# A record-counting kernel: tiles of 384 rows in four slots in place of 512 rows in three, and the last batch's pieces summed before one matmul

## The chip, the cores and the metric

The kernel runs on one core of a Trainium2 chip. The metric is the device time of one execution in microseconds (us). A core has five engines that run their own instruction queues and meet at semaphores: TensorE (PE, matmuls into PSUM), VectorE (DVE), ScalarE (ACT), GpSimd (POOL) and SyncE (SP), which here issues nearly all transfers. The transfers themselves run on 16 DMA engines.

## The reference

```python
B, S, D = 8, 2048, 4096          # x is [B, S, D], w is [D, 1], all float32

def reference(x, w):
    proj = (x @ w).squeeze(-1)
    cm = np.maximum.accumulate(proj, axis=1)
    is_record = (proj >= cm).astype(np.float32)
    return np.cumsum(is_record, axis=1).astype(np.float32)
```

Every row of x (4096 values, 16 KB) is reduced to one dot product with w. Along S, a running maximum says which dot products are records, and a running count of the records is the output, [8, 2048]. x is 268 MB and is read once; everything else is small.

## The kernel before

**Rows in tiles.** The first 1920 of the 2048 positions are worked off in four groups, of 4, 4, 4 and 3 times 128 positions (`RS`, lines 42 to 50). A group has eight tiles, one for each batch, from batch 7 down to batch 0. A tile of a four-row group is 128 partitions by four rows of x, which lie one after the other in memory: 64 KB for each partition, 8 MB in all. In the last group a tile has three rows: 48 KB and 6 MB. The tiles go through `NS` = 3 slots of `xall` (line 81), each wide enough for four rows; tile t of a group uses slot t % 3, in every group anew. All loads are issued by SyncE in one queue, in program order (lines 154 to 173). A load waits, by the semaphore `fr` of the earlier user of its slot, until VectorE and ScalarE are both through with that tile; `user_before` (lines 147 to 150) says which one it is: for t >= 3 the tile t - 3 of the same group, for t < 3 the last tile of the group before that used the same slot, which is tile 6, 7 or 5 for t = 0, 1 or 2.

**Work on a tile.** The columns of a row are split. VectorE takes the first 2816 (`VC`), a multiply with a running sum in one instruction per row (`dot`, line 120; `group_dots`, line 240). GpSimd multiplies the other 1280 with w in place (`group_products`, line 263), and ScalarE adds them up (`add_up`, line 126; `group_sums`, line 278). GpSimd starts on a tile when VectorE has seen it land (`go`). The two partial results of a row and batch are columns of `sum_v` and `sum_p`.

**End of a group.** TensorE turns the columns of both sums into rows of PSUM (`ps`, lines 295 to 305), which adds them at the same time: a matmul with the identity, for each row of the tile one for `sum_p` and one for `sum_v`, once all eight tiles are done. VectorE then runs three instructions (`scans`, line 135): a running maximum from `ps` to `cm`, the comparison (which overwrites `ps`), and a running sum to `cnt`. They stand at the start of the next group's VectorE program (`group_scans`, line 235); a first pass before the first group works on filler values. The loops of VectorE, GpSimd and ScalarE are hardware loops over the first three groups, with the last group written out behind them. The counts of a group are stored from SyncE's queue behind the next group's fifth load (lines 170 to 173).

**The last 128 positions** are loaded as single rows (16 KB for each partition, 2 MB), one for each batch. Batches 7 to 2 are whole rows (`rows`); batches 1 and 0 are cut into nine pieces of columns that get smaller towards the end (`PIECES`, lines 56 to 66). Rows 0 to 2 of this tail go into the fourth row of the three slots, which the last group doesn't use, rows 3 to 5 into the slot of the last group's tile 5, and the pieces into that of tile 6 (`slot`, line 175). The store of the last group's counts stands between the fourth and the fifth piece, and waits for that group's scans. VectorE runs the tail's first dot product, then the last group's scans, then the rest (lines 326 to 338).

**The last matmuls** (lines 340 to 357): three turn the results of batches 7 to 1, and one for each partial result of a piece of batch 0 turns that column (7 from VectorE, 2 from ScalarE), all added in one row set of `ps`. Each matmul waits for its own operand; the two from ScalarE are moved towards the end of the order. A float32 matmul shows as two passes in the profile. Then come the last `scans`, over 128 columns, and the last store.

Of the kernel before, what the change touches and what calls it, by code (L numbers as in the profile page):

```python
# [20 lines left out]
def kernel(  # L21
# [17 lines left out]
    B, S, D = x.shape  # L39
    WC = 512  # L40
    NW = D // WC
    RS = (4, 4, 4, 3)
    R = RS[0]
    NS = 3
    NG = len(RS)
    NL = NG - 1
    N = R * P
    STARTS = [sum(RS[:g]) * P for g in range(NG)]
    S0 = sum(RS) * P
    assert S0 + P == S  # L50
    VC = 2816
    PC = D - VC
    CV = 3584
# [27 lines left out]
    xbuf = [xall[:, i * R * D : (i + 1) * R * D] for i in range(NS)]  # L81
    w_sb = sb([P, PC], "w_sb")
    cm = sb([B, N], "cm")
    cnt = sb([B, N], "cnt")
    cm_l, cnt_l = (sb([B, P], n) for n in ("cm_l", "cnt_l"))
    w_v = wpool.tile([P, CV], FP32, name="w_v")
    ps = wpool.tile([P, WC], FP32, name="ps")
    w_row = w2[:NW, :]
# [8 lines left out]
    sum_v, sum_p = cut(R * B), cut(R * B)  # L97
    st_v, st_p = cut(B), cut(B)
    b1x = cut(B)
    acc_v = cut(len(PIECES))  # L100
    acc_p = cut(len(PIECES))
    neg = cut(1)[:B]

    ns = iter(range(1000))

    def sem(name):
        return tc.alloc_semaphore(f"{name}_{next(ns)}")

    rows = [b for b in reversed(range(B)) if b > 1]
    xs = [sem("xs") for _ in range(B)]  # L110
    fr = [sem("fr") for _ in range(B)]
    xt = [sem("xt") for _ in rows]
    xq = [sem("xq") for _ in PIECES]
    ws, idn, bw, wc, cs, od, oe, psr, pd, pl, go, sd, pa, con = (
# [17 lines left out]
        assert W2 <= c0 and c1 <= W2 + WC  # L132
        return w2[:, c0 - W2 : c1 - W2]

    def scans(cm_, cnt_, n, cm0, cnt0, base=1):
        low = neg.to_broadcast([B, n])
        V.tensor_tensor_scan(  # L137
            out=cm_, data0=ps[:B, :n], data1=low, initial=cm0, op0=ALU.max, op1=ALU.max,
        )._wait_ge(psr, base).then_inc(psr, 1)
        V.tensor_tensor(  # L140
            out=ps[:B, :n], in0=ps[:B, :n], in1=cm_, op=ALU.is_ge
        )._wait_ge(psr, base + 1).then_inc(psr, 1)
        V.tensor_tensor_scan(  # L143
            out=cnt_, data0=ps[:B, :n], data1=low, initial=cnt0, op0=ALU.add, op1=ALU.max,
        )._wait_ge(psr, base + 2).then_inc(cs, 1)

    def user_before(g, t):
        if t >= NS:
            return t - NS, g + 1
        return max(u for u in range(B) if u % NS == t), g  # L150

    with tc.tile_critical(no_gpsimd_drain=True):  # L152

        for g in range(NG):
            r = RS[g]
            for t in range(B):
                i = SY.dma_start(
                    out=xbuf[t % NS][:, : r * D],
                    in_=x[B - 1 - t, STARTS[g] : STARTS[g] + r * P, :].rearrange(
                        "(p r) d -> p (r d)", r=r  # L160
                    ),
                ).then_inc(xs[t], 16)
                u, n = user_before(g, t)
                if n:
                    i._wait_ge(fr[u], 2 * n)
                if g == t == 0:
                    A.dma_start(
                        out=w_row, in_=w.rearrange("(k c) one -> k (c one)", k=NW)
                    ).then_inc(ws, 16)
                if t == 4 and g:  # L170
                    SY.dma_start(
                        out=out[:, STARTS[g - 1] : STARTS[g]], in_=cnt
                    )._wait_ge(cs, g + 1).then_inc(od, 16)

        def slot(m):
            if m < NS:
                return None, xbuf[m][:, RS[-1] * D :]
            u = B - NS if m < 2 * NS else B - NS + 1
            return u, xbuf[u % NS][:, (m % NS) * D : (m % NS + 1) * D]

        freed = {None}

        def row_load(m, c0, c1, b, done):
            u, xb = slot(m)
            i = SY.dma_start(  # L185
                out=xb[:, c0:c1], in_=x[b, S0:, c0:c1]
            ).then_inc(done, 16)
            if u not in freed:
                freed.add(u)
                i._wait_ge(fr[u], 2 * NG)  # L190

        for m, b in enumerate(rows):
            row_load(m, 0, D, b, xt[m])
        for i, (b, c0, c1, _, _) in enumerate(PIECES):
            row_load(B - 1 - b, c0, c1, b, xq[i])
            if i == 3:
                SY.dma_start(
                    out=out[:, STARTS[-1] : S0], in_=cnt[:, : S0 - STARTS[-1]]
                )._wait_ge(cs, NG + 1).then_inc(oe, 16)


# [28 lines left out]
        V.memset(cnt[:, N - 1 :], 0.0)  # L230
        V.wait_ge(con, 3)
        V.wait_ge(wc, 3)
        V.memset(ps[:B, :N], LOW).then_inc(psr, 1)  # L233

        def group_scans(r=R):
            V.wait_ge(od, 16)
            n = r * P
            scans(cm[:, :n], cnt[:, :n], n, cm[:, N - 1 :], cnt[:, N - 1 :])

        def group_dots(r):  # L240
            for t in range(B):
                b, s = B - 1 - t, t % NS
                V.wait_ge(xs[t], 16).then_inc(go, 1)
                V.sem_inc(xs[t], -16)  # L244
                for j in range(r):
                    i = dot(
                        xbuf[s][:, j * D : j * D + VC], w_v[:, :VC],
                        sum_v[:, j * B + b : j * B + b + 1],
                    )
                i.then_inc(fr[t], 1)  # L250

        def next_group():
            group_scans()
            V.sem_inc(psr, -3)
            V.sem_inc(od, -16)

        with V.Fori(0, NL):
            next_group()
            group_dots(R)
        next_group()  # L260
        group_dots(RS[-1])

        def group_products(r):
            for t in range(B):
                s = t % NS
                for j in range(r):
                    xl = xbuf[s][:, j * D + VC : (j + 1) * D]
                    i = G.tensor_mul(out=xl, in0=xl, in1=w_sb).then_inc(pl, 1)  # L268
                    if j == 0:
                        i._wait_ge(go, 1)  # L270
                G.sem_inc(go, -1)  # L271

        G.wait_ge(wc, 3)
        with G.Fori(0, NL):  # L274
            group_products(R)
        group_products(RS[-1])

        def group_sums(r):
            for t in range(B):
                b, s = B - 1 - t, t % NS  # L280
                for j in range(r):
                    i = add_up(
                        xbuf[s][:, j * D + VC : (j + 1) * D],
                        sum_p[:, j * B + b : j * B + b + 1],
                    )._wait_ge(pl, j + 1)
                i.then_inc(fr[t], 1)
                A.sem_inc(pl, -r)
            A.wait_ge(pd, 1)
            A.sem_inc(pd, -1)

        with A.Fori(0, NL):
            group_sums(R)
        group_sums(RS[-1])

        for g, r in enumerate(RS):
            for j in range(r):
                for k, l in enumerate((sum_p, sum_v)):
                    i = T.matmul(  # L298
                        out=ps[:B, j : r * P : r], lhsT=l[:, j * B : (j + 1) * B],
                        rhs=identity, start=k == 0, stop=k == 1,  # L300
                    )
                    if j == k == 0:
                        i._wait_ge(fr[B - 1], 2 * (g + 1))
                    if j == r - 1:
                        i.then_inc((pd, psr)[k], 1)


# [18 lines left out]
        for m, b in enumerate(rows):  # L326
            piece(
                slot(m)[1], (0, VC), (VC, D), st_v[:, b : b + 1], st_p[:, b : b + 1],
                xt[m],
            )  # L330
            if m == 0:
                group_scans(RS[-1])
        for i, (b, c0, c1, v, p) in enumerate(PIECES):
            if b == 1:
                dst_v, dst_p = (b1x if p is None else st_v)[:, 1:2], st_p[:, 1:2]
            else:
                dst_v, dst_p = acc_v[:, i : i + 1], acc_p[:, i : i + 1]
            piece(slot(B - 1 - b)[1], v, p, dst_v, dst_p, xq[i])
            if i == 1:
                parts += [(B, st_v, (sd, nv)), (B, b1x, None), (B, st_p, (pa, na))]  # L340
            elif b == 0:
                parts.append((1, dst_v, (sd, nv)))
                if p:
                    parts.append((1, dst_p, (pa, na)))

        a0 = next(i for i, q in enumerate(parts) if q[2] == (pa, na - 1))
        a1 = next(i for i, q in enumerate(parts) if q[2] == (pa, na))
        parts.insert(len(parts) - 2, parts.pop(a1))
        parts.insert(len(parts) - 4, parts.pop(a0))
        for k, (m, l, wait) in enumerate(parts):  # L350
            i = T.matmul(  # L351
                out=ps[:m, :P], lhsT=l[:, :m], rhs=identity,
# [2 lines left out]
            if wait:  # L355
                i._wait_ge(*wait)
        i.then_inc(psr, 1)
        n = RS[-1] * P
        scans(cm_l, cnt_l, P, cm[:, n - 1 : n], cnt[:, n - 1 : n], 4)
        SY.dma_start(out=out[:, S0:], in_=cnt_l)._wait_ge(cs, NG + 2).then_inc(oe, 16)  # L360
        G.wait_ge(oe, 16 * 2)

# [29 lines left out]
```

## Time and profile before

| what | value |
|---|---|
| median of 8 runs (lowest, highest) | 633.08 us (632.11, 633.44) |
| the profiled execution, its own time | 632.51 us |
| its span, first to last instruction | 630.6 us |
| HBM read over the span | 268.45 MB, 426 GB/s with writes |
| busy: VectorE / GpSimd / ScalarE / PE | 406.0 / 368.8 / 177.7 / 31.9 us |
| loads of four rows, issue to landing (median of the 24) | 44.9 us |
| mean granted TensorE clock | 0.647 |

In the profile, L121 is line 121 of the kernel; that of a helper stands for all its calls, so L121 is every dot product of VectorE and L127 every sum of ScalarE. The granted clock is the share of full speed that TensorE was allowed. The slices cut the span into 40 equal parts and give a busy share in tenths. The chain of waits goes back from the last instruction, at each step to what released it; "issue" in it is time in which the engine waited for nothing that the profile shows. The costliest groups of instructions read: line, engine, operation, written operand, read operands, shapes and count, then busy time and the mean of one in ns, then idle time before and what ended it:

```profile
L121 DVE CUSTOM_DVE_ANT_0 xall<-xall,w_v 128x2816 f32<-128x2816 f32 (+3 forms) x135 | 388.7, 2932 | 189.5 <-DVEq L244 187.4
L268 POOL TENSOR_TENSOR xall<-xall,w_sb 128x1280 f32<-128x1280 f32 x120 | 344.8, 2906 | 248.0 <-POOLq L271 248.0
L127 ACT ACTIVATE xall<-xall 128x1280 f32<-128x1280 f32 x129 | 162.6, 1261 | 432.6 <-POOL xall L268 414.6
```

VectorE and GpSimd each wait some 190 to 250 us in all for tiles (the lines named after the arrow are the semaphore steps that follow a landing), ScalarE for GpSimd's products.

### The profile page before, as it was taken

What the parts mean: (1) busy time and instruction counts of PE and PEld (TensorE: products, weight loads), DVE (VectorE), ACT (ScalarE), POOL (GpSimd) and SP (SyncE); (2) the same over time, 40 slices, a digit from 0 to 9 for tenths busy, and PEclk for the clock granted to TensorE, in tenths of its full rate; (3) what the DMA queues carried; (4) which work ended last, traced back from release to release, by engine and by line L of the source; (5) the groups of instructions that cost most, each with busy time, mean ns of one, the idle gap of its engine ahead of it and who ended that gap; (6) DMA issues with size and microseconds to landing.
All of it is one profiled execution on the core that took longest, in us unless ns stands there. A gap on an engine that the chain in (4) does not pass through costs nothing.

```text
span 630.6 us, 1174 instructions
## 1 busy us (share of the span) xinstructions
PE 31.9 (5%) x100; PEld 14.4 (2%) x100; DVE 406.0 (64%) x291; ACT 177.7 (28%) x262; POOL 368.8 (58%) x137
## 2 busy tenths in 40 slices
PE   8000000000010000000020000000002000000102
PEld 3000000000000000000010000000001000000001
DVE  0755676556785557755579655577557866655797
ACT  1222332123322223322233222332222332232242
POOL 0555676455765557755567655577555766555865
PEclk9999999999965555555555555555556555555556
DMA  9999999999999999999999999999999999999996
GB/s 400 399 466 412 453 399 466 400 466 399 466 412 453 428 436 449 417 453 412 457 407 461 403 466 399 467 399 466 399 459 396 409 446 446 406 446 446 403 428 242
DMA packets 6869, 268.57 MB, mean 426 GB/s; under 512 B 800, under 2 KB 1328, under 8 KB 1872
## 3 DMA queue, kind: packets, MB, share of 16 engines
q1 hardware_dynamic: 6848, 268.50, 98.8%
q14 instruction: 4, 0.03, 0.0%
q8 instruction: 1, 0.02, 0.0%
q10 hardware_dynamic: 16, 0.02, 0.0%
HBM read 268.45 MB, written 0.07 MB: 426 GB/s over the span
## 4 chain that ended last, share of the span: by engine, by line
POOL 52%; issue 37%; DMA 7%; PE 3%; DVE 1%; SPq 0%; POOLq 0%; ACT 0%; ACTq 0%
POOL xall L268 52%; DMA xall<-in_x_dram 6%; PE w_v L215 2%; DVE xall L121 0%; PE ps L215 0%; PE ps L351 0%; DMA w<-in_w_dram 0%; SPq L185 0%; POOLq L271 0%; ACT w L225 0%; DVE cm_l L137 0%; DVE cnt_l L143 0%; DVE ps L140 0%; ACT xall L127 0%; POOLq L274 0%
## 5 line engine op out<-in xcount | busy, mean ns | idle before, releaser
L121 DVE CUSTOM_DVE_ANT_0 xall<-xall,w_v 128x2816 f32<-128x2816 f32 (+3 forms) x135 | 388.7, 2932 | 189.5 <-DVEq L244 187.4
L268 POOL TENSOR_TENSOR xall<-xall,w_sb 128x1280 f32<-128x1280 f32 x120 | 344.8, 2906 | 248.0 <-POOLq L271 248.0
L127 ACT ACTIVATE xall<-xall 128x1280 f32<-128x1280 f32 x129 | 162.6, 1261 | 432.6 <-POOL xall L268 414.6
L298 PE MATMUL ps<-identity,small 128*8 128x128 f32 x60 | 13.2, 412 | 569.1 <-ACT xall L127 569.1
L319 POOL TENSOR_TENSOR xall<-xall,w_sb 128x1280 f32<-128x1280 f32 (+1 forms) x8 | 22.1, 2766 | 6.8 <-DMA xall<-in_x_dram 6.7
L127 ACT ACTIVATION_READ_ACCUMULATOR xall<-xall 128x1 f32 x129 | 24.0, 186 | 0.0
L298 PEld LDWEIGHTS ps<-identity,small 128*8 128x8 f32 x60 | 7.5, 130 | 575.9 <-ACT xall L127 572.0
L137 DVE TENSOR_TENSOR_SCAN cm<-ps,cm,small 8x512 f32<-8x512 f32 (+1 forms) x5 | 6.1, 1217 | 13.2 <-PE ps L298 13.2
L215 PE MATMUL w_v<-w,identity 8*128 8x512 f32 x14 | 12.1, 1056 | 0.0
L233 DVE MEMSET ps<- 8x512 f32 x1 | 0.5, 485 | 17.2 <-ACT w L225 17.2
L121 DVE DVE_READ_ACCUMULATOR2_ANT small<- 128x1 f32 x135 | 11.0, 81 | 0.0
L143 DVE TENSOR_TENSOR_SCAN cnt<-ps,cnt,small 8x512 f32<-8x512 f32 (+1 forms) x5 | 6.1, 1217 | 0.2
L351 PE MATMUL ps<-identity,small 128*1 128x128 f32 (+1 forms) x24 | 4.7, 351 | 23.0 <-DVE small L121 23.0
L215 PEld LDWEIGHTS w_v<-w,identity 8*128 8x128 f32 x14 | 4.6, 332 | 7.3 <-issue 7.3
L222 ACT COPY w_sb<-w_v 128x768 f32<-128x768 f32 x1 | 0.8, 799 | 11.4 <-PE w_v L215 11.4
L140 DVE TENSOR_TENSOR ps<-ps,cm 8x512 f32<-8x512 f32 (+1 forms) x5 | 3.3, 660 | 0.2
L351 PEld LDWEIGHTS ps<-identity,small 128*1 128x1 f32 (+1 forms) x24 | 1.8, 93 | 26.2 <-DVE small L121 25.2
L215 PE MATMUL ps<-w,identity 8*128 8x512 f32 x2 | 2.1, 1136 | 2.7 <-DMA w<-in_w_dram 2.7
L221 ACT ACT_TABLE_LOAD x1 | 1.3, 1283 | 1.5 <-SPq L152 1.5
L221 ACT COPY w_sb<-ps 128x512 f32<-128x512 f32 x1 | 0.6, 586 | 2.0 <-PE ps L215 2.0
L137 DVE TENSOR_TENSOR_SCAN cm_l<-ps,cm,small 8x128 f32<-8x128 f32 x1 | 0.5, 470 | 0.7 <-PE ps L351 0.7
L319 POOL TENSOR_TENSOR xall<-xall,w 128x320 f32<-128x320 f32 x1 | 0.9, 863 | 0.0
(14 smaller groups left out, 3.4 us busy)
## 6 DMA issues: line engine op xcount, KB each, us to landing
xall<-in_x_dram SPq DMA_DIRECT2D x8, 6144.0 KB, 32.6
xall<-in_x_dram SPq DMA_DIRECT2D x6, 2048.0 KB, 42.5
xall<-in_x_dram SPq DMA_DIRECT2D x1, 1344.0 KB, 36.8
xall<-in_x_dram SPq DMA_DIRECT2D x2, 384.0 KB, 30.6
xall<-in_x_dram SPq DMA_DIRECT2D x1, 704.0 KB, 38.2
xall<-in_x_dram SPq DMA_DIRECT2D x1, 640.0 KB, 39.2
xall<-in_x_dram SPq DMA_DIRECT2D x24, 44.9
xall<-in_x_dram SPq DMA_DIRECT2D x1, 224.0 KB, 21.9
```

The lines of the kernel that those rows point to most:

```text
L121: return V.tensor_tensor_reduce(out=xsl, in0=xsl, in1=wsl, scale=1.0, scalar=0.0, op0=ALU.mult, op1=ALU.add, accum_out=dst,)
L127: return A.activation(out=xsl, in_=xsl, func=ACTF.Copy, accum_out=dst)
L137: V.tensor_tensor_scan(out=cm_, data0=ps[:B, :n], data1=low, initial=cm0, op0=ALU.max, op1=ALU.max,)._wait_ge(psr, base).then_inc(psr, 1)
L140: V.tensor_tensor(out=ps[:B, :n], in0=ps[:B, :n], in1=cm_, op=ALU.is_ge)._wait_ge(psr, base + 1).then_inc(psr, 1)
L143: V.tensor_tensor_scan(out=cnt_, data0=ps[:B, :n], data1=low, initial=cnt0, op0=ALU.add, op1=ALU.max,)._wait_ge(psr, base + 2).then_inc(cs, 1)
L215: i = T.matmul(out=dst, lhsT=identity[:NW, k : k + 1].to_broadcast([NW, P]), rhs=w_row, start=True, stop=True,).then_inc(bw, 1)
L221: A.copy(out=w_sb[:, CV - VC :], in_=ps)._wait_ge(bw, 1).then_inc(wc, 1)
L222: A.copy(out=w_sb[:, : CV - VC], in_=w_v[:, VC:CV])._wait_ge(bw, NW).then_inc(wc, 1)
L268: i = G.tensor_mul(out=xl, in0=xl, in1=w_sb).then_inc(pl, 1)
L298: i = T.matmul(out=ps[:B, j : r * P : r], lhsT=l[:, j * B : (j + 1) * B], rhs=identity, start=k == 0, stop=k == 1,)
L319: G.tensor_mul(out=xl, in0=xl, in1=w_pool(*p))._wait_ge(landed, 16).then_inc(pl, 1)
L351: i = T.matmul(out=ps[:m, :P], lhsT=l[:, :m], rhs=identity, start=k == 0, stop=k == len(parts) - 1,)
```

## The change

Three things are changed.

1. Tiles have three rows (48 KB for each partition, 6 MB) in all groups, of which there are five, and go through four slots. Tile k of all 40 uses slot k % 4; since eight tiles are a multiple of four, the slot follows from t alone, and a load always waits for the load four back. `xs` and `fr` are one semaphore for each slot. All five groups are passes of the hardware loops. The tail's rows 0 to 2 go into slot 0, rows 3 to 5 into slot 1, the pieces into slot 2.
2. In `scans`, the comparison writes a tile of its own in SBUF (`rec`, `rec_l`) instead of `ps`, and the running sum adds to each element a zero that lies in the last column of `ps`, in place of a maximum with a very low number.
3. The partial results of batch 0's pieces lie in one array, `accs` (18 columns, those not used are zero). VectorE adds them up with one instruction into `fin` after the last piece, and one matmul turns `fin`. In front of the last piece's dot product VectorE waits for ScalarE's last sum.

```diff
-    RS = (4, 4, 4, 3)
-    R = RS[0]
-    NS = 3
-    NG = len(RS)
+    R = 3
+    NS = 4
+    NG = (S - P) // (R * P)
...
+    rec = sb([B, N], "rec")
...
-    acc_v = cut(len(PIECES))
-    acc_p = cut(len(PIECES))
+    accs = cut(2 * len(PIECES))
+    acc_v, acc_p = accs[:, : len(PIECES)], accs[:, len(PIECES) :]
+    fin = cut(1)
     neg = cut(1)[:B]
+    zero = ps[:B, WC - 1 :]
...
         V.tensor_tensor(
-            out=ps[:B, :n], in0=ps[:B, :n], in1=cm_, op=ALU.is_ge
+            out=rec_, in0=ps[:B, :n], in1=cm_, op=ALU.is_ge
         )._wait_ge(psr, base + 1).then_inc(psr, 1)
         V.tensor_tensor_scan(
-            out=cnt_, data0=ps[:B, :n], data1=low, initial=cnt0, op0=ALU.add, op1=ALU.max,
+            out=cnt_, data0=rec_, data1=zero.to_broadcast([B, n]), initial=cnt0,
+            op0=ALU.add, op1=ALU.add,
         )._wait_ge(psr, base + 2).then_inc(cs, 1)
...
+        for k in range(NK):
+            g, t = divmod(k, B)
+            i = SY.dma_start(
+                out=xbuf[k % NS],
+                in_=x[B - 1 - t, g * N : (g + 1) * N, :].rearrange(
+                    "(p r) d -> p (r d)", r=R
+                ),
+            ).then_inc(xs[k % NS], 16)
+            if k >= NS:
+                i._wait_ge(fr[k % NS], 2 * (k // NS))
...
+            if t == NS and g:
+                SY.dma_start(
+                    out=out[:, (g - 1) * N : g * N], in_=cnt
+                )._wait_ge(cs, g + 1).then_inc(od, 16)
...
         def slot(m):
-            if m < NS:
-                return None, xbuf[m][:, RS[-1] * D :]
-            u = B - NS if m < 2 * NS else B - NS + 1
-            return u, xbuf[u % NS][:, (m % NS) * D : (m % NS + 1) * D]
+            return m // R, xbuf[m // R][:, (m % R) * D : (m % R + 1) * D]
...
-        with V.Fori(0, NL):
-            next_group()
-            group_dots(R)
-        next_group()
-        group_dots(RS[-1])
+        with V.Fori(0, NG):
+            group_scans()
+            V.sem_inc(psr, -3)
+            V.sem_inc(od, -16)
             for t in range(B):
...
+            if i == len(PIECES) - 1:
+                V.wait_ge(pa, na)
             piece(slot(B - 1 - b)[1], v, p, dst_v, dst_p, xq[i])
...
-            elif b == 0:
-                parts.append((1, dst_v, (sd, nv)))
-                if p:
-                    parts.append((1, dst_p, (pa, na)))
-
-        a0 = next(i for i, q in enumerate(parts) if q[2] == (pa, na - 1))
-        a1 = next(i for i, q in enumerate(parts) if q[2] == (pa, na))
-        parts.insert(len(parts) - 2, parts.pop(a1))
-        parts.insert(len(parts) - 4, parts.pop(a0))
+        V.tensor_reduce(
+            out=fin, in_=accs, op=ALU.add, axis=mybir.AxisListType.X
+        )._wait_ge(sd, nv).then_inc(sd, 1)
+        nv += 1
+        parts.append((1, fin, (sd, nv)))
+
```

The loops of GpSimd and ScalarE and the matmuls of a group are changed in the same way: one loop over five groups of three rows, and `fr[NS - 1]` as the matmuls' wait.

## The prediction

> **What bounds the kernel now.** I read the slices of the span first, then the DMA queues, then the chain of waits.
>
> ```profile
> DVE  0755676556785557755579655577557866655797
> POOL 0555676455765557755567655577555766555865
> DMA  9999999999999999999999999999999999999996
> q1 hardware_dynamic: 6848, 268.50, 98.8%
> ```
>
> The load queue occupies the 16 DMA engines for 98.8% of the span (third number), in every slice but the last. VectorE and GpSimd stand near six tenths. So the time is 268.5 MB at the rate of the loads, plus a start, plus what follows the last byte; a saving on any engine counts only in that last part, and one on the queue counts in full. Next I read the chain as a clock of landings: GpSimd's first product of a tile starts as soon as VectorE has seen the tile land (but for a group's first tile, 487.17 here, which waits for VectorE's scans).
>
> ```profile
> 216.98 11.50 POOL xall L268 x4
> ...
> 236.28 11.50 POOL xall L268 x4
> ...
> 487.17 8.62 POOL xall L268 x3
> ...
> 499.05 8.63 POOL xall L268 x3
> ...
> 513.59 8.62 POOL xall L268 x3
> ...
> 571.64 8.63 POOL xall L268 x3
> ```
>
> (Start, length.) Four-row tiles come 19.30 us apart (216.98 to 236.28). From 178.39 to 294.31 in the same view it is 115.92 / 6 = 19.32, with one store of counts in it: 4.830 us per row of 2 MB. Three-row tiles: (571.64 - 499.05) / 5 = 14.518, also with one store: 4.839 per row. Two places don't fit. The first three-row tile and the second together take 499.05 - 468.26 = 30.79 (468.26 is the start of the tile before), where 2 x 14.52 = 29.04 is due: 1.75 us lost. And the steps from 80.97 to 100.63 and to 120.50 are 19.66 and 19.87: 0.89 us lost.
>
> For the first I looked at the sync engine's issues, in order of time, and at the issuing line in a window around each:
>
> ```profile
> 481.18 0.81 SPq L157 DMA_DIRECT2D xall<-in_x_dram  x2
> ```
> ```profile
> L157 SPq DMA_DIRECT2D xall<-in_x_dram x1: 328/328/328, 481.2 to 481.2; - x1
> ...
> DMA to landing us min/median/max: 17.8/17.8/17.8
> ```
>
> Loads 25 and 26 (counting from 0) are issued only at 481.18, one right after the other, and 25 lands at 481.2 + 17.8 = 499.0. Load 24, issued at 461.9 with 20.8 to landing in the same view, landed at 482.7. So 25 came 16.3 after it instead of 14.5. Alone, without a queue ahead, a load takes its bytes' time and some 3 us more: 17.8 - 14.5 = 3.3 here, and 21.9 - 19.3 = 2.6 for the first one of all (issued at 0.95). Here only 482.7 - 481.2 = 1.5 of that was covered: 3.3 - 1.5 = 1.8 lost. The reason for the late issue is in the code: eight tiles go round three slots, starting at slot 0 in every group, so the tile t = 1 of a group takes the slot of t = 7 of the group before, two loads back instead of three. That tile (start 468.26) is free 12.92 us later, at 481.18, while load 24, now three rows long, is through in 14.5. At the other boundaries the same issue comes as late (172.02, to landing 25.6 = 6.3 + 19.3), but there 6.3 us of a load of 19.3 are still to come: the step 178.39 to 197.69 is 19.30. So a cover of 1.5 us failed and one of 6.3 held. The end of the chain is the other part:
>
> ```profile
> 622.72 0.95 DVE xall L121
> ...
> 624.99 1.74 PE ps L351 x12
> 626.73 0.02 issue
> 626.75 0.48 DVE cm_l L137
> ```
>
> VectorE works off the last column pieces back to back from 622.72; its last dot product (160 columns) starts at 625.70, its result is read out by 626.02, and the PE, which has matmuls of earlier pieces in front, lets the scan start at 626.75, 0.73 later.
>
> **The change part by part.** The profiled execution took 632.51 us: a span of 630.6 and 1.9 around it. The median of the runs is 633.08, 0.57 more; I add my sum to the median.
>
> *Slots.* Four slots of three rows, and 8 tiles are a multiple of 4: every load waits for the load four back, across groups too. A three-row tile is free 10.04 us after its start (513.58 to the issue at 523.62). By then the load in progress has 14.5 - 10.0 = 4.5 us to go and two more are queued, 29 us: a margin of 33. At a group's end VectorE is held by the PE's row (2.73) and the scans (599.03 to 601.66, 2.63), so a tile may start its dots some 1 us after landing, and a loop that starts late does it once (VectorE is ready near 21.5, as before, with the first tile landed near 18); 33 covers these. The loss of 1.75 goes: **-1.75**. Bounds: 0 if the cause is another, -1.75.
>
> *Size of a load.* 24 loads of four rows, 96 row-units, become 32 of three: 96 x (4.839 - 4.830) = **+0.9**. Bounds from the single steps: 14.49 / 3 = 4.830 against 19.32 / 4 gives 0; 14.55 / 3 = 4.850 against 19.29 / 4 = 4.823 gives +2.6. The Trainium skill, DMA: Bandwidth & Descriptors, "Anatomy of one DMA — SWDGE (gpsimd) path", has a fixed 2.0 us for each DMA that GpSimd issues, besides its bytes; if eight more loads paid it in the open, this term would be an estimated +16. The steps here (sync-engine loads) show 0.01 us per row, so queued loads cover it. More issues cost the sync engine 8 x 0.33 us, in waits of over 10 us.
>
> *Stores of counts.* One more inside the stream (four, not three). The steps that hold one are 19.41 (255.59 to 275.00) against 19.31: **+0.1**, 0 to 0.1. The store stands in the sync queue behind a group's fifth load, as before, and waits for scans that precede the tile which that load waited for: nothing behind it is later.
>
> *The disturbed steps at 81 to 120 us* have no late issue and nothing else that the change touches: kept, 0 (to -0.89 if they go).
>
> *Scans.* Six of 384 columns in place of four of 512 and one of 384; the comparison writes SBUF, the second scan adds a zero from PSUM. All but the last set lie under the stream, in the 33 us. The last set is on the path, 0.47 + 0.29 + 0.47. No row prices the other memory; I take 0, with 0.15 either way, the fixed part of the comparison (8x384 0.554, 8x128 0.286: 1.05 ns a column and 0.15).
>
> *The end.* Nine late matmuls (eighteen passes) go; a sum over 18 columns and one matmul (two passes) come. By the comparison's line the sum is 0.15 + 18 x 0.00105 = 0.17; bounds 0.08 (reading out an accumulator, 81 ns) and 0.29 (the comparison over 128). From the read-out: 0.04 to the next VectorE instruction (as between scan and comparison), 0.17, 0.06 to the PE, two passes, 0.03 to the scan. Two passes took 0.59 at half clock (start 624.35 to 624.94) and 0.38 at full clock (625.46 to 625.84). The granted clock was 0.5 until about 625.5, and the new matmul comes after more than 3 us of idle PE: 0.59. Sum 0.89 against 0.73: **+0.16** (-0.14 to +0.28). The added wait before the last dot product is for ScalarE's last sum, which ends at 625.17; that dot product starts at 625.70, so it costs nothing; behind it stand the last dot, the sum and the scans, which would move one for one if it came later.
>
> *Loops.* All groups now are loop passes, and the exit lies just before the last rows instead of a group earlier. In the trace the exits and returns hide behind the wait for the PE (VectorE's first scan waits 4.29 for it). Taken as 0, with the VectorE's idle time in the tail, 1.5 + 0.3 + 0.2 = 2.0 us, as cover. The Trainium skill, Runtime: NRT & Kernel Launch, "Instruction fetch mechanics", warns that a taken branch to a page outside the fetched window stalls the engine; it gives no time, and the returns at 178 and 333 show none.
>
> Sum: -1.75 + 0.9 + 0.1 + 0.16 = -0.6, so 633.08 - 0.6 = **632.5 us**. The last rows and pieces are loaded in the same order into as many rows: before, three slots with tiles of three rows and the three spare rows; now four slots of three. Their waits (26 us in all, two of them, in the sync queue's waits) are for the third-last and second-last tile in both, and the first three rows, which had no wait of their own behind a load that waits for the fourth-last tile, now wait for that tile.
>
> **Rivals.**
> *Faster.* The loss goes, the disturbed steps were the long loads' own or chance, and the row price is equal: -1.75 - 0.89 + 0.1 + 0.16 = -2.4: 630.7. For it: the single steps overlap (4.830). Against: the means don't, and the disturbed steps have no cause in the code.
> *The stall is not the slot order.* If it comes with something that stays, such as the code behind the loops, the sum is +0.9 + 0.1 + 0.16 = +1.2: 634.2. Against: the 17.8 to landing, as from rest. The row's upper price (+2.6) with the stall gone gives +1.1, the same place.
> *Slower: the exit of the loop in the tail.* VectorE leaves the loop after the last tile (near 595 now), with rows landing every 4.84 and its own work at 3.0 each, and it catches up only at 613.6, 1.5 us before the row it then waits for. A stall D moves the end by D - 2.0; with 5 us, 3.0 - 0.6 = +2.4: 635.5. It decides from D = 3.9. For it: nothing in the old trace shows an exit without cover. Against: an engine's queue runs ahead of its work; GpSimd's branch out of the loop is at 468.37 in the chain, the products before it end at 479.75.
>
> **How the numbers follow.** A measurement of this kernel tells about 0.2%, 1.3 us, from no change: under 631.8 is faster, over 634.3 slower. Forecast 0.58: with the row term at its ends the sum is -1.5 or +1.1, so 0.06 of it falls below the lower line, 0.02 above the upper, 0.50 between. Faster rival 0.18, all of it faster. Stall kept 0.08, at the upper line: 0.04 on each side. Loop exit 0.16: 0.13 slower, and 0.03 for a stall that its cover nearly holds. Faster 0.24, same 0.57, slower 0.19. The range goes down to the faster rival's 630.7, and up to the line where the stall kept ends, 634.4; it leaves out the loop exit's 0.13 and a few hundredths below.
>
> **What would show it.** Right: three-row steps of 14.52 throughout, loads that land some 48 us after issue (4 x 14.52 less the 10 that a tile is in use; now 44.9), the DMA share above 98.8%, one reduction of 0.1 to 0.3 us, and a scan starting about 0.9 after the last read-out. Wrong: an issue that follows the landing of the load before it, steps over 14.6, or idle VectorE gone between 601 and 622.

## The result

| | median us (runs) | lowest to highest |
|---|---|---|
| before | 633.11 (32) | 632.11 to 634.18 |
| changed | 631.32 (12) | 631.20 to 631.81 |

The ratio is 0.9974, interval 0.9966 to 0.9981: 1.8 us faster, where 0.6 was forecast. The time lies in the range (630.7 to 634.4), which reached so low for the faster rival alone, and beyond the 0.2% that the likeliest case stayed within. The profiled execution of the changed kernel took 631.31 us, with a span of 629.2.

From the page of the changed kernel, the queues and the loads:

```profile
q1 hardware_dynamic: 8016, 268.50, 98.8%
...
q14 instruction: 2, 0.02, 0.0%
...
xall<-in_x_dram SPq DMA_DIRECT2D x40, 6144.0 KB, 47.8
```

The DMA engines are as busy as before (98.8%, where a higher share had been expected), and a load lands 47.8 us after its issue (44.9 before, for loads of four rows), as worked out from four slots. A line on "instruction" counts packets of code that the engines loaded while the kernel ran. The page of before has two such lines:

```profile
q14 instruction: 4, 0.03, 0.0%
q8 instruction: 1, 0.02, 0.0%
```

The four are 8 KB each and fall among the loads. The single one is 16 KB, at 625.3 us, just behind the last landing; of the kernels here, those with the old end or with added matmuls written out have it.

The chain of waits of the changed kernel (start, length), at the places shown of before:

```profile
483.07 8.62 POOL xall L253 x3
...
497.28 8.63 POOL xall L253 x3
...
511.78 8.63 POOL xall L253 x3
```

Steps of 14.2 (483.07 is a group's first tile, late by VectorE's scans) and 14.50. The step of 16.3 between two landings is gone, and of the long steps near 100 us (19.66 and 19.87 before) one of 14.64 is left. The chain's end:

```profile
623.91 0.23 DVE xall L121
624.14 0.02 DVE small L121
624.16 0.02 issue
624.19 0.18 DVE small L319
624.37 0.04 issue
624.41 0.60 PE ps L326 x2
625.01 0.02 issue
625.04 0.48 DVE cm_l L136
```

After the last dot product is read out (624.15) come the sum (L319), two passes of the PE and the scan, at 625.04: 0.89 us, the number that was worked out. Before, that stretch was 0.73 in the profile shown.

The last load landed at 625.31 before and at 623.47 now, 1.84 earlier. From there to the end it is 5.75 us, where it was 5.33: 0.13 of the difference lies ahead of the last scan, 0.3 between the last store's issue and the program's end. The spans differ by 1.4 us and the medians by 1.8, since the profiled execution of before lies 0.6 below its kernel's median (632.51 against 633.11) and that of the changed kernel on it. The terms of the sum don't come out: -1.75 + 0.9 + 0.1 puts the last landing 0.75 earlier, and it came 1.84 earlier. The experiments take the change apart.

### The profile page after: what moved, and what is told of

It is laid out like the page before. It is cut to its first block, busy times and chain, and to the rows that moved or that the text cites. A ratio compares the mean times of both kernels' runs of the same rounds, so it can differ in the third digit from the quotient of the medians.

```text
span 629.2 us, 1209 instructions
## 1 busy us (share of the span) xinstructions
PE 29.9 (5%) x84; PEld 13.0 (2%) x84; DVE 406.4 (65%) x296; ACT 177.8 (28%) x262; POOL 369.1 (59%) x137
## 3 DMA queue, kind: packets, MB, share of 16 engines
q1 hardware_dynamic: 8016, 268.50, 98.8%
## 4 chain that ended last, share of the span: by engine, by line
POOL 53%; issue 39%; DMA 4%; PE 3%; DVE 1%; POOLq 0%; ACT 0%; SPq 0%; ACTq 0%
POOL xall L253 53%; DMA xall<-in_x_dram 3%; PE w_v L207 2%; DMA w<-in_w_dram 0%; PE ps L274 0%; DVE xall L121 0%; PE ps L207 0%; DVE cm L136 0%; DVE cnt L143 0%; POOLq L256 0%; PE ps L326 0%; ACT w L217 0%; DVE rec L140 0%; DVE cm_l L136 0%; DVE cnt_l L143 0%
## 5 line engine op out<-in xcount | busy, mean ns | idle before, releaser
L136 DVE TENSOR_TENSOR_SCAN cm<-ps,cm,small 8x384 f32<-8x384 f32 x6 | 6.0, 1004 | 15.0 <-PE ps L274 14.9
L143 DVE TENSOR_TENSOR_SCAN cnt<-rec,cnt,ps 8x384 f32<-8x384 f32 x6 | 6.0, 1001 | 0.2
L326 PE MATMUL ps<-identity,small 128*8 128x128 f32 (+1 forms) x8 | 2.2, 405 | 25.6 <-DVE small L121 22.8
L140 DVE TENSOR_TENSOR rec<-ps,cm 8x384 f32<-8x384 f32 x6 | 3.3, 546 | 0.2
## 6 DMA issues: line engine op xcount, KB each, us to landing
xall<-in_x_dram SPq DMA_DIRECT2D x40, 6144.0 KB, 47.8
```

What stands on the lines that cost most here:

```text
L136: V.tensor_tensor_scan(out=cm_, data0=ps[:B, :n], data1=neg.to_broadcast([B, n]), initial=cm0, op0=ALU.max, op1=ALU.max,)._wait_ge(psr, ba ...
L140: V.tensor_tensor(out=rec_, in0=ps[:B, :n], in1=cm_, op=ALU.is_ge)._wait_ge(psr, base + 1).then_inc(psr, 1)
L143: V.tensor_tensor_scan(out=cnt_, data0=rec_, data1=zero.to_broadcast([B, n]), initial=cnt0, op0=ALU.add, op1=ALU.add,)._wait_ge(psr, base ...
L326: i = T.matmul(out=ps[:m, :P], lhsT=l[:, :m], rhs=identity, start=k == 0, stop=k == len(parts) - 1,)
```

## The experiments

Three chips were used, and each kernel was timed against the kernel before on the same chip; the ratio is to that. Its median there was 632.91 (for `slots`, `again`, `end_only` and `tiles_old_end`), 632.76 (for `unrolled`, `slots_new_end` and the two `warm` kernels) and 633.03 (for the two `loop` kernels and `after_again`). Intervals of the ratios are 0.0009 to 0.0012 wide on each side, 0.6 us or more, so of two experiments only differences above that are sure by time alone; smaller ones rest on the traces.

### Only the slots of the last group (`slots`)

```diff
+    def at(g, t):
+        return (t + (2 if g == NL else 0)) % NS
...
+        if g == NL:
+            return B - NS + t, g
...
-                    out=xbuf[t % NS][:, : r * D],
+                    out=xbuf[at(g, t)][:, : r * D],
```

The engines' programs of the last group and the tail's rows take their slots from `at` as well.

> Only the slots of the last group are changed, against the kernel before: its tiles go on round the three slots (tile t in slot (t + 2) % 3), so each of its loads waits for the tile three loads back. Loads keep four rows. If the late issue is the cause of the 1.75 us: 633.1 - 1.8 = 631.3, the second three-row tile follows the first by 14.5 us, and its load is issued some 13 us earlier and takes over 25 us to landing. If the loss belongs to something else at that place (the first load of another size, the code behind the loops): 633.1, and the step stays at 16.3. If the steps at 81 to 120 us that were 0.9 too long belong to long loads, they may come again here and the times stay scattered over some 2 us; if not, the times lie within 0.6 us, as those of the changed kernel.

Measured: 632.02 us (631.26 to 632.40), ratio 0.9984 (0.9975 to 0.9993): 0.9 less, half of what was expected. The issuing line in a window around the load that was late, and the chain of waits:

```profile
L162 SPq DMA_DIRECT2D xall<-in_x_dram x1: 327/327/327, 461.8 to 461.8; - x1
...
DMA to landing us min/median/max: 35.3/35.3/35.3
```
```profile
497.17 8.63 POOL xall L273 x3
...
511.66 8.63 POOL xall L273 x3
```

The load is issued at 461.8, not 481.2, and takes 35.3 us to landing, not 17.8: queued in time. It lands at 497.1, 14.5 after the one before it, so the late issue was the cause of the step of 16.3. The runs of `slots` fall into two groups, five from 631.26 to 631.52 with a mean granted clock of 0.771 to 0.893 and six from 632.02 to 632.40 with 0.644 to 0.648; the old end is the likely reason (see `tiles_old_end`). The kernel before has that end too, and from lowest run to lowest run the gain is 0.88 as well, so the groups don't account for the missing half. It is lost later. GpSimd's products in order of time (start, length; in brackets the idle time before and its cause), in the tail's rows of this kernel:

```profile
598.76 2.91 POOL L324 TENSOR_TENSOR xall<-xall,w_sb 128x1280 f32<-128x1280 f32 x1 [0.16 <-DMA xall<-in_x_dram]
604.60 2.90 POOL L324 TENSOR_TENSOR xall<-xall,w_sb 128x1280 f32<-128x1280 f32 x1 [2.93 <-DMA xall<-in_x_dram]
609.45 2.90 POOL L324 TENSOR_TENSOR xall<-xall,w_sb 128x1280 f32<-128x1280 f32 x1 [1.95 <-DMA xall<-in_x_dram]
```

One row comes 5.84 after the last, where 4.85 is due: 1.0 us lost, though all these loads had been issued almost 40 us before they landed. The trace's transfers show a packet of code at 602.6 there, and the 16 semaphore increments of each load show what it does. (By the Trainium skill, DMA: Bandwidth & Descriptors, "Why a DMA increments its semaphore by 16 and not by 1", each of the engines that share a DMA adds one when its part has landed; the sixteen times here fit that: sorted, they keep nearly the same spacing from load to load. Which engine a time belongs to isn't recorded.) At this row the middle of the sixteen times goes on by 4.88, while the last falls from 0.85 to 1.81 us behind the middle and is still 1.70 behind at the end. A load has landed when the last of the sixteen has. Read in this way, the last load of each kernel (each from one profile):

| kernel | middle engine | last engine | behind | packets of code in the stream, at us |
|---|---|---|---|---|
| before | 624.50 | 625.31 | 0.81 | 107.0, 116.8, 491.9, 604.6 |
| `again` (before, unchanged) | 624.38 | 625.15 | 0.77 | 104.5, 116.5, 491.6, 604.6 |
| `end_only` | 624.12 | 624.91 | 0.79 | 106.7, 116.4, 491.7, 604.4 |
| `slots` | 622.51 | 624.21 | 1.70 | 104.4, 116.5, 492.3, 602.6 |
| `slots_new_end` | 622.29 | 623.92 | 1.63 | 106.6, 116.3, 492.0, 602.3 |
| changed | 622.66 | 623.47 | 0.81 | 97.0, 118.9 |
| `after_again` | 622.64 | 623.63 | 0.99 | 95.4, 118.8 |
| `unrolled` | 622.76 | 625.27 | 2.50 | 109.8, 118.8, 182.1, 313.8, 380.5, 532.2 |
| `warm_new_end` | 622.68 | 623.76 | 1.08 | 95.3, 118.9, and 16 KB at 620.2 |
| `loop_new_end` | 622.62 | 623.55 | 0.94 | 95.3, 119.0 |

For the middle engine the slots are worth 2.0 us; for the last one, 1.1. The second pair of kernels that differ by the slots alone, `end_only` and `slots_new_end`, says the same: 1.83 and 0.99. In the three profiles with the stop at 482 us, the packet near 604 raises an engine that isn't the last (the last time goes from 0.98 to 0.92 behind in the kernel before, and another rises from under 0.3 to 0.63); in the two without it, the packet near 602 hits the one that is furthest behind. That the stop, in which the queue ran dry, decides which engine is behind would fit this, but it isn't shown: the increments name no engine, and no run tried it by itself.

### The kernel before again (`again`)

> The kernel before, unchanged, for a second profile. The step from the first three-row tile to the second should be 16.3 again, since the issue is late by the program. If the steps at 81 to 120 us are bound to the loads' addresses, the same ones are too long again; if they are chance, all are 19.3 there, or others are long.

One run, 632.72 us. The same step is 16.2 again (482.55 to 498.78), and the step to the sixth tile's landing, at 120.28, is long again: 20.02. In `slots`, `slots_new_end` and `end_only` it is 20.06, 19.86 and 19.86. So this step is neither chance nor the loads' own: it comes with the packets of code near 105 and 117 us, with which the last engine falls 0.35 to 0.74 us further behind. The other long step, the 19.66 to 100.63, does not come again (19.32 here). It ended before the first packet, at 107.0, and all sixteen engines were late in it, so it isn't code; it fits chance, and its cause stays open. In the changed kernel the step to 105.58 is 14.64, 0.14 too long (14.81 in `after_again`).

### The loops written out (`unrolled`)

```diff
-        with V.Fori(0, NG):
+        for _ in range(NG):
```

On VectorE, GpSimd and ScalarE of the changed kernel alike.

> The changed kernel with the loops of VectorE, GpSimd and ScalarE written out, which changes the code alone: the same instructions without branches. If the exit and the returns of the loops cost nothing, as predicted, and the loading of code neither, 631.3. If each block of code that is loaded while the rows stream in holds up one of the 16 DMA engines, and the last load waits for the engine that is furthest behind, more blocks are loaded, the landings of one engine lie up to 1 us or more behind the rest, and the time is 631.5 to 632.5, with more scatter.

Measured: 633.07 us (632.84 to 633.29), ratio 1.0002: the whole gain is lost, with the same tiles, slots and end. The chain of waits, and the page's line of the code's packets:

```profile
294.25 8.63 POOL xall L253 x3
...
308.74 8.62 POOL xall L253 x3
...
324.27 8.63 POOL xall L253 x3
...
338.76 8.63 POOL xall L253 x3
```
```profile
q14 instruction: 6, 0.05, 0.0%
```

Steps of 14.49, then 15.53, then 14.49: 1.0 lost around the packet at 313.8. It happens once more at 532.2 (527.21 to 542.68, 15.47), each time, by the spacing of the sixteen, to the engine that is furthest behind, which ends 2.50 behind the middle; the changed kernel's last is 0.81 behind. The other four packets cost the landings far less: the one at 380.5 puts back, by over 0.7, an engine that isn't the last, and with the first three the last engine falls back by under 0.2. The difference, 1.69, is that of the times, 1.75. The packet of 8 KB itself takes 0.3 us of the engine; what makes it 1.0 isn't shown. With all engines full, little of it comes back: 1.66 us behind after the first of the two, 1.55 before the second, over 200 us later.

### The new end alone (`end_only`), and the old end in the changed kernel (`tiles_old_end`)

```diff
+        V.tensor_reduce(
+            out=fin, in_=accs, op=ALU.add, axis=mybir.AxisListType.X
+        )._wait_ge(sd, nv).then_inc(sd, 1)
```

This, its matmul and its wait are put into the kernel before, or taken out of the changed one.

> The kernel before with the new end alone (the sum into one column and one matmul, and the wait before the last piece). By the same working 633.1 + 0.16 = 633.3; a change of under 0.3 us either way. If the end is where the 1.8 us came from, 631.5.

> The changed kernel with the old end: one matmul for each partial result of batch 0 in place of the sum and one matmul. If the new end costs 0.16 us, as worked out, this takes 631.3 - 0.16 = 631.15, and the last scan starts 0.73 after the last read-out in place of 0.89. If the new end saves time, it takes over 631.4.

Measured: `end_only` 632.36 us, ratio 0.9994 (0.9985 to 1.0003), no change that can be told. `tiles_old_end` 631.67 us (631.31 to 632.28), ratio 0.9984 (0.9975 to 0.9993), where 631.15 was expected: more than the changed kernel, not less. Its runs fall into two groups, six from 631.31 to 631.67 and five from 632.05 to 632.28. Its profile is of one at 632.25; engines in order of time:

```profile
623.13 2.77 PE L327 MATMUL ps<-identity,small 128*1 128x128 f32 x12
...
624.09 0.08 DVE L121 DVE_READ_ACCUMULATOR2_ANT small<- 128x1 f32 x1
625.94 0.47 DVE L136 TENSOR_TENSOR_SCAN cm_l<-ps,cm,small 8x128 f32<-8x128 f32 x1 [1.77 <-PE ps L327]
```

The last read-out ends at 624.17, the scan starts 1.77 later: twelve passes of the PE take 2.77 us and stand in line, the last of them 0.21 us apart. In the profile of before, the same twelve took 1.74 and the wait was 0.73: its passes are 0.21 apart, too, up to 625.46, where the granted clock goes from 0.5 to 1.0, and 0.11 from there on. So 0.21 is the half clock. (The mean clock on record for `tiles_old_end`, 0.999, doesn't tell: its trace holds no change of clock before 626.02.) In `again` the clock rises at 626.25 and the wait is 1.18. The PE's 16 KB of code, which all three load between 624 and 626.6, are not the reason: the passes follow one another without a gap. The price of the old end was read from its best case.

### The PE kept busy (`warm_old_end`, `warm_new_end`, `loop_old_end`, `loop_new_end`)

```diff
+        T.wait_ge(sd, len(rows))
+        for _ in range(12):
+            T.matmul(
+                out=ps[:B, N : N + 124], lhsT=identity[:, :B], rhs=identity[:, :124],
+                start=True, stop=True,
+            )
```

In the two `loop` kernels the second line is `with T.Fori(0, 12):`.

> The changed kernel with the old end (a matmul for each partial result), and twelve matmuls more on the idle PE, from the sixth row's dot product on, whose results nothing reads (columns 384 to 507 of the PSUM row set). Without them this kernel's times fell into two groups, 631.3 to 631.7 and 632.05 to 632.3, and the profile of one at 632.25 shows matmul passes at half clock up to the end and the last scan 1.77 us after the last read-out. If the clock of the PE is what parts them, all runs now lie near 631.2 and the scan starts about 0.7 after the read-out. If not, the two groups stay.

> The changed kernel with the same twelve matmuls. If the clock counts here too, the one last matmul takes 0.38 in place of 0.59, the last scan starts 0.68 after the last read-out in place of 0.89, and the time is 631.32 - 0.2 = 631.1. If the clock is at full speed by now or doesn't matter, no change; if the added matmuls hold up the first three of the end, it gets slower.

> The changed kernel with the old end and the same loop. If the half clock is what makes the old end slow in some runs, they all have the last scan some 0.73 after the last read-out: 631.3 less 0.16, so 631.15, in one group, unless the PE's block of code, which this kernel loads near 624, now falls among the last pieces and adds up to 1 us. If not the clock, two groups again, 631.4 and 632.2.

> The changed kernel with the twelve unread matmuls again, now as a loop of the PE, which is a few instructions of code and not 48. Written out, they brought the scan to 0.68 us after the last read-out, but the PE loaded 16 KB of code at 620 us, on one DMA engine among the last pieces, and the time was 631.97. If that load is what cost the time, it is gone here, the last landing is some 623.5 again and the time 631.32 - 0.2 = 631.1. If the matmuls themselves cost it, 631.9 again.

Measured, written out: 631.96 (old end, 631.51 to 632.40) and 631.97 (new end, 631.51 to 632.66): no gain. The scan did come early, 0.73 and 0.68 after the read-out, but with the added instructions the PE loads 16 KB of code at 620.2 us in both, among the pieces (at 624.0 in `tiles_old_end`, not at all in the changed kernel), and the last landing was at 623.86 and 623.76 (623.47 and 623.63 in two profiles of the changed kernel). These profiles are of a run within 0.01 us of the fastest of each; what made the others up to 1.1 us slower isn't shown. As a loop: 631.31 (old end, 630.98 to 631.53, ratio 0.9970, 0.9959 to 0.9982) and 631.26 (new end, 631.07 to 631.54, ratio 0.9973, 0.9962 to 0.9984). The old end's two groups have become one, of 0.55 us (on another chip), though its profile, of the slowest of these runs, has the block of code at 622.8 and the last landing at 623.83. The end of `loop_old_end`:

```profile
623.94 0.96 PEld L333 LDWEIGHTS ps<-identity,small 128*1 128x1 f32 x10 [0.39 <-DVE small L121]
...
624.42 0.08 DVE L121 DVE_READ_ACCUMULATOR2_ANT small<- 128x1 f32 x1
625.23 0.47 DVE L136 TENSOR_TENSOR_SCAN cm_l<-ps,cm,small 8x128 f32<-8x128 f32 x1 [0.73 <-PE ps L333]
```

Ten weight loads take 0.96 us here; in `tiles_old_end` they took 1.79 (same count, same form). And `loop_new_end`:

```profile
624.15 0.08 DVE L121 DVE_READ_ACCUMULATOR2_ANT small<- 128x1 f32 x1
624.26 0.17 DVE L319 TENSOR_REDUCE small<-small 128x1 f32<-128x18 f32 x1
...
624.49 0.38 PE L332 MATMUL ps<-identity,small 128*1 128x128 f32 x2 [1.45 <-DVE small L319]
624.91 0.47 DVE L136 TENSOR_TENSOR_SCAN cm_l<-ps,cm,small 8x128 f32<-8x128 f32 x1 [0.47 <-PE ps L332]
```

Two passes in 0.38 in place of 0.59, and the scan 0.68 after the read-out. Against the changed kernel on the same chip (631.45) that is 0.19 less, as expected, but within what the runs can't tell apart.

### Slots and new end, loads of four rows (`slots_new_end`)

Both edits above in the kernel before.

> The kernel before with the slots of its last group changed and with the new end, loads still of four rows: from the changed kernel it differs by the size of the loads, the loops and the code that goes with them, and the scans. If smaller loads cost the 0.9 us that was worked out, this takes 631.3 - 0.9 = 630.4. If they cost nothing, it takes 631.3, like the changed kernel. More of its runs may lie some 0.5 to 1 us higher than of the changed kernel, if the two further blocks of code that it loads while the rows stream in hold up one DMA engine.

Measured: 631.68 us (631.11 to 632.12), ratio 0.9978 (0.9969 to 0.9987). Neither 630.4 nor 631.3: by the table its middle engine is through 0.37 earlier than the changed kernel's, its last one 0.45 later. Loads of four rows are a little better; the packet of code at 602.3, which the changed kernel doesn't have, takes more than that back (the last engine falls from 0.75 to 1.69 behind).

### The changed kernel again (`after_again`)

> The changed kernel, unchanged, beside the others on the same chip: 631.3, and less than 0.7 us between its runs if the old end's clock is what scatters the others. If other runs of it scatter by over 1 us too, the scatter is the chip's.

Measured: 631.45 us (631.10 to 631.69, ratio 0.9976, 0.9966 to 0.9986), all runs within 0.6 us.

## Why the prediction was right or wrong

**Right.** The stream of loads is the bound. The late issue at the last group's second load was the cause of the step of 16.3 (`slots`: queued in time, 14.5), and the rival that kept the stall falls. So does the slower one. The margin of four slots held: 47.8 us to landing. The new end takes 0.89 from read-out to scan, its sum 0.17, both as worked out. The exit of the loop in the tail costs VectorE nothing that shows: it waits 1.61 us for the sixth row's landing, 1.54 before. The direction was right; the size, 1.8 for 0.6, was not.

**Slots, -1.75.** The stop was of that size (1.8 in the landings), and for the middle DMA engine the slots are worth 2.0, but the last engine gained 1.1 and the time 0.9 (`slots`): without the stop, a packet of code put the last engine 0.96 further behind.

**Size of a load, +0.9: mis-sized.** The table gives +0.37 for the middle engine between `slots_new_end` and the changed kernel, with the added store and the other scans in it. The steps it was taken from, 4.839 and 4.830 us per row, differ by a hundredth of a microsecond, times 96; the three-row one came from after the stop and with other loads behind it, and the changed kernel's is 14.50 / 3 = 4.833.

**"The disturbed steps ... have no late issue and nothing else that the change touches: kept, 0", and "Loops ... Taken as 0": the steps that failed.** The disturbed step to 120.50 is code being loaded, and the change touches that most of all: with all groups in loops there are two packets of code in the stream where there were four. `unrolled` shows the price the other way, +1.75 for six. Between `slots_new_end` and the changed kernel the last engine is 0.82 less behind. Against the kernel before it is level (0.81 in both), so the loops don't add to the slots' gain; they keep it from being lost, as `slots` loses it. The prediction sought the cost of loops at the engines that run them, where none shows; it lies on a DMA engine. The faster rival had the gain of these steps in it, but put it down to the long loads or to chance, which fits the step to 100.63 alone.

**The end, +0.16: right for the profile of before, wrong for its runs.** That profile had the PE at full clock from 625.46 on. In two other profiles the old end is 0.45 and 1.04 slower, and the new one, with one matmul after the sum, differs by 0.2 between the clocks (0.89 and 0.68). By the medians it saves 0.35 in the changed kernel (631.67 to 631.32) and 0.55 in the old one, each less than the runs can tell for sure. That the clock parts the groups rests on the spacing of the passes in these profiles and on the single group of `loop_old_end`; no run of the lower group of `tiles_old_end` was profiled.

Added up by medians: slots -0.9, new end -0.35, three-row tiles with their code -0.35, together -1.6 of the -1.8. The last two are each below the 0.6 us that the times alone can tell.

The Trainium skill's rule on taken branches (Runtime: NRT & Kernel Launch, "Instruction fetch mechanics") speaks for writing loops out. Here it is the other way round: 631.32 with loops, 633.07 without. The same section's remark that a block boundary's cost is mostly hidden fits what the chain of `unrolled` shows of GpSimd (8.63 us for a tile's products, as elsewhere), but not the DMA engine that carries the code, where `unrolled` lost 1.0 us each at 313.8 and 532.2.

## What to carry to other kernels

Where all DMA engines are full to the end, whatever takes the one that is furthest behind, code too, delays the last landing; here loops were worth more than their branches cost. The removal of a stop in such a stream can gain less than the stop's length, when another delay then counts. A price read from one profile of a short burst on the PE holds for the clock of that run; compare the passes' durations in a second profile before a difference of some tenths is counted.

## What was not expected of the hardware

A packet of 8 KB of code takes 0.3 us of a DMA engine, but that engine's share of the loads comes up to 1.0 us later (`unrolled`, at 313.8 and 532.2; `slots`, at 602.6), and only 0.1 of the delay is made up in the 200 us that follow. Twenty-four added passes on the idle PE, written out, made it load 16 KB of code among the last pieces, and the kernel took 0.65 us more (631.97, on another chip) in spite of the 0.21 that the clock gained; as a loop they cost nothing that can be seen (631.26).
